# Two steps change places in a decoder kernel: a doubling step ahead of the window's value product, the queries' state product ahead of the second block's inverse

## The chip, the cores and the metric

The kernel runs on one core of a Trainium2 chip. The metric is the device time of one execution in microseconds (us). An execution has a span, from its first to its last recorded instruction, and a little more time around it. The engines are named as in the profile: PE is the matrix engine (TensorE), PEld its loading of stationary operands, DVE the VectorE, ACT the ScalarE, POOL the GpSimd, SP the engine that issues the weight DMAs.

## The reference, cut to what matters

Two layers are computed over 256 tokens of width 1024. Each layer is a half-step SwiGLU, a group of three token mixers that run on the same normalised stream, an output projection and a second half-step SwiGLU, with a layer norm after each. The mixers are a gated DeltaNet, a sliding-window attention with sinks, and a cross-attention to a memory. Their outputs are weighted by sigmoid gates and added:

```python
o_dn = deltanet_branch(dn_q, dn_k, dn_v, dn_b, dn_a, dn_z, ...)
o_sw = sliding_window_attention(sw_q, sw_k, sw_v, swa_sinks)
o_xa = memory_cross_attention(xa_q, mem_n, w_mem_kv)
gates = jax.nn.sigmoid(gates.reshape(B_, S_, N_BRANCH, D))
merged = jnp.sum(gates * jnp.einsum('bsnc,ncd->bsnd', branches, w_branch), axis=2)
```

Two pieces of this matter here. The sliding-window attention multiplies its softmax weights by the values (`o = einsum(p, vb)`). The DeltaNet solves a unit triangular system for every chunk and head and carries a state `S` from chunk to chunk: `v_new = u - w S`, `o = q S + qk v_new`.

## The kernel before, in words

All large products are made from float32 numbers split in two parts. A weight unit of 128 x 1024 arrives by DMA in a tile `raw`; ScalarE rounds it to `whi`, VectorE makes the rest `wlo` (both line 125, in `split`), and three matmuls (line 134, through `mm3`) use `whi` twice and `wlo` once. Four `raw` buffers and five each of `whi` and `wlo` let the conversions run ahead of PE.

Within a mixer group PE's matmuls are pinned to program order (`pinned[0] = True`; products have line 134 in the profile, transposes line 137). That order is written out by hand: `weave(work, steps)` runs a generator of large products, here `gates(n)` (a gate projection in eight steps, each of one weight unit and 12 matmuls) or `branch(n, o)` (a branch projection in four steps), and after step k calls the small pieces that stand under k in a table. The order on DVE and ACT is chosen by a scheduler, the DMA queue of SP keeps program order, and waits between engines follow from the tiles that are shared.

The tokens are handled as two blocks of 128. The small pieces that the change and its steps touch are these:

- `w_scores(tb, hh)` makes the window's scores of one block and half of the heads in `at` banks (a ring of two PSUM banks); DVE reads each bank at line 779 into a tile `pp`, then maximum (785), exponentials on ACT (791), sums (792, 793) and scaling (794). `w_turn` transposes the weights and copies them to `pt` (804).
- `w_values(0)` multiplies the first block's weights `pt` by the values `swv` into one `at` bank (the rows `at<-pt,swv` on PE), and `split` moves it to the two parts of `oS` (ACT and DVE at line 125, the rows `u<-at`).
- `inverses()` builds 16 x 16 inverses on POOL (lines 845 to 847). `begin_inverse` transposes the result on DVE (line 940).
- `doubling(c)` is a generator for each block c that makes larger inverses out of smaller ones; `double()` advances both by one step. The first step is 64 matmuls of 32 x 32 in two `sm` banks (the rows `sm<-w,l`; a ring of two banks as well), each bank copied by ACT at line 884; the second subtracts at line 890 on DVE.
- `rec_v0`, `rec_s1`, `rec_r1`, `rec_o0`, `rec_qs`, `rec_v1`, `rec_o1` are the recurrence: each is four matmuls of 128 x 128 (eight records in the trace) in an `sm` bank and an eviction. `rec_r1` leaves R1 by four DVE operations at line 983; `rec_v1` multiplies the second block's inverse by R1 and is copied by ACT at line 990; `rec_qs` multiplies the queries by the state S1, and DVE evicts it at line 987; `rec_o1` uses V1, and DVE adds it at line 994.

Of the kernel before, what the change touches and what calls it, by code (L numbers as in the profile page):

```python
# [38 lines left out]
def tile_trunk(ctx, tc, x, xT, mem, memT_, wst, lnp, memln, cvw, rows, cst, out):  # L39
# [22 lines left out]
    def T(pool, shape, tag, dt=F32, bufs=None):  # L62
        pool = pn if pool is pu and tag in NEAR else pool
        kw = {} if bufs is None else {"bufs": bufs}
        return pool.tile(shape, dt, tag=tag, name=nm(tag), **kw)
# [4 lines left out]
    def at():  # L70
        return T(psT, [P, 512], "at")
# [52 lines left out]
    def split(hi, lo, src):  # L124
        return nc.scalar.copy(hi, src).ins, nc.vector.tensor_tensor(lo, src, hi.bitcast(F32), op=ALU.subtract).ins  # L125
# [7 lines left out]
    def matmul(*a, **k):  # L133
        return pe(nc.tensor.matmul(*a, **k))  # L134
# [10 lines left out]
    def weave(work, steps):  # L145

        for n, _ in enumerate(work, 1):
            for f in steps.get(n, ()):
                f()
# [374 lines left out]
    def mixers(l, hT, mkT, mv_, post):  # L524
# [281 lines left out]
        def w_values(tb):  # L806
            if not oS:
                oS.extend(T(pu, [P, 4, S], tag, F32R) for tag in ("u6", "u7"))
            ts = slice(tb * P, (tb + 1) * P)
            pso = at()  # L810
            for kb in range(tb + 1):
                for kv in range(2):
                    hs = slice(kv * 64, kv * 64 + 64)
                    matmul(pso[hs, :], swv[:, kb, hs], wpT[tb][kb][:, kv].rearrange("p h q -> p (h q)"), start=kb == 0, stop=kb == tb)
            late["act"], late["dve"] = split(oS[0][:, :, ts], oS[1][:, :, ts], pso.rearrange("p (h k) -> p h k", h=4))
# [189 lines left out]
        def gates(n):  # L1005
            gt = gts[n] = [T(p2, [P, D], "gt") for _ in range(2)]
            for j in range(2):
                js = slice(j * 512, (j + 1) * 512)
                outs = [acc() for _ in range(2)]
                for uu in range(KD // 2):  # L1010
                    hi, lo = unit()
                    for tb in range(2):
                        ts = slice(tb * P, (tb + 1) * P)
                        for kk in range(2):
                            k, c = 2 * uu + kk, slice(kk * 512, kk * 512 + 512)
                            mm3(outs[tb], (xt[0](k)[:, ts], xt[1](k)[:, ts]), (hi[:, c], lo[:, c]), k == 0, k == KD - 1)
                    if uu < KD // 2 - 1:
                        yield
                for tb in range(2):
                    nc.scalar.activation(gt[tb][:, js], outs[tb], AF.Tanh, scale=0.5)  # L1020
                yield

        def branch(n, o):
# [27 lines left out]
            3: [lambda: w_turn(0, 1), begin_inverse],  # L1051
            4: [lambda: w_scores(1, 0)]})
        weave(gates(1), {
            1: [lambda: w_values(0), double],
            2: [lambda: w_scores(1, 1)],
            3: [double, lambda: held(leave_v)],
            5: [double, lambda: w_turn(1, 0), lambda: held(back_v)],
# [7 lines left out]
            4: [rec_r1]})  # L1065
        weave(gates(2), {
            1: [rec_o0],
            2: [rec_v1, rec_qs],
            3: [rec_o1],
            5: [lambda: finish_turn(0)],  # L1070
            8: [lambda: finish_turn(1)]})
# [59 lines left out]
    for l in range(NL):  # L1131
        mT = []
        mid = memory_T(mT, l)
        if l == 0:

            mid[2] = lambda: load(cs, cst)
            more = {4: lambda *a: xres(0), 6: lambda *a: xres(1), 8: lambda *a: small()}
        post = Post(lnp[l, 0, 0], lnp[l, 0, 1])
        f1.rest(hT, 4, [((pu, "u0"), (pu, "u1")), ((pu, "u2"), (pu, "u3"))], post, mid, ends, {} if l else more)
        kv = memory_kv(mT, post.end)  # L1140
        if l == 0:
            nc.scalar.activation(nea, rw[:, :, 8:12], AF.Exp)
            nc.vector.tensor_scalar(nea, nea, -1.0, None, ALU.mult)
        post2 = Post(lnp[l, 1, 0], lnp[l, 1, 1])
        mixers(l, post.hT, *kv, post2)
        f2 = Ffn()
        begin(f2, post2.hT)
        last = l == NL - 1
        post = Post(lnp[l, 2, 0], lnp[l, 2, 1], last)
        f2.rest(post2.hT, 6, [((pu, a), (pu, b)) for a, b in (("u0", "u1"), ("u2", "u3"), ("u4", "u5"), ("u6", "u13"))], post, behind=post2.end)  # L1150
        ends = post.end
        if not last:
            f1, hT = Ffn(), post.hT
            begin(f1, hT)
# [87 lines left out]
```

## Time and profile before

| | |
|---|---|
| median of 3 runs | 1271.19 us (1271.11 to 1272.05) |
| profiled execution, its own time | 1271.84 us |
| its span | 1270.1 us |
| mean granted clock of TensorE | 0.999 |
| DVE, ACT, POOL busy | 69%, 52%, 17% |
| DMA | 263.56 MB, mean 208 GB/s |

A row of the timeline gives the start of an instruction or of a run of equal ones, how long it took, engine, line, operation, output and inputs by the program's names, shape and count, and in brackets how long the engine sat idle before it and what ended that. Matmuls overlap: the next one starts before the row of the last one ends, so that distances on PE are read from start to start. The small pieces of the change stand once in each layer, at about 340 and 395 us in the first layer and at about 970 and 1025 us in the second.

### The profile page before, as it was taken

The numbers are of one execution on the slowest core, as the hardware profiler recorded it, in microseconds if no ns is written. First come the engines' busy times: TensorE is split into PE (matmuls) and PEld (weight loads), VectorE is DVE, ScalarE is ACT, GpSimd is POOL, SyncE is SP. The second block draws the span as 40 slices with busy tenths as digits, with TensorE's granted clock in tenths as the row PEclk, the third lists the DMA queues.
The fourth block names the chain that finished last, engine by engine and source line by source line (L and its number), as shares of the span: only waits on it lengthen the run. The fifth ranks groups of instructions, "written<-read, shape, count | busy, mean of one in ns | idle before, by whom it ended". The sixth has DMA issues, their size and how long they took to land.

```text
span 1270.1 us, 18774 instructions
## 1 busy us (share of the span) xinstructions
PE 1258.1 (99%) x6916; PEld 1070.9 (84%) x6916; DVE 871.3 (69%) x1284; ACT 661.5 (52%) x982; POOL 221.0 (17%) x395
## 2 busy tenths in 40 slices
PE   9999999999999999999999999999999999999997
PEld 7888889999878888888888888899987788888886
DVE  6678576886667776665666665759776588766565
ACT  6456444655664544454454554455646654454441
POOL 1233000002331102221012220000023401122100
PEclk9999999999999999999999999999999999999999
DMA  8988765655554648787668887566554456578771
GB/s 293 322 265 286 249 210 160 205 179 137 164 151 150 240 139 258 243 242 220 215 208 246 256 255 216 178 185 212 162 158 133 134 189 226 174 248 243 240 231 74
DMA packets 78795, 263.56 MB, mean 208 GB/s; under 512 B 12528, under 2 KB 13968, under 8 KB 78704
## 3 DMA queue, kind: packets, MB, share of 16 engines
q1 hardware_dynamic: 66320, 232.40, 56.5%
q0 software_dynamic: 12240, 29.84, 8.7%
q8 instruction: 54, 0.88, 0.3%
q14 instruction: 37, 0.30, 0.1%
q10 hardware_dynamic: 144, 0.13, 0.0%
HBM read 247.48 MB, written 14.85 MB: 207 GB/s over the span
## 4 chain that ended last, share of the span: by engine, by line
PE 94%; DVE 3%; DMA 2%; ACT 1%; issue 1%; SPq 0%; DVEq 0%; ACTq 0%
PE acc L134 83%; PE at L134 3%; PE sm L134 3%; DMA raw<-in_wst_dram 2%; PE sm L137 1%; DVE wlo L125 1%; PE acc L335 1%; PE acc L332 1%; PE at L137 1%; PE acc L333 1%; ACT whi L125 1%; DVE h L291 0%; DVE h L296 0%; DVE h L418 0%; DVE bnst L277 0%
## 5 line engine op out<-in xcount | busy, mean ns | idle before, releaser
L125 DVE TENSOR_TENSOR wlo<-raw,whi 128x1024 fp32r<-128x1024 f32 (+2 forms) x405 | 487.1, 1210 | 277.0 <-ACT whi L125 275.0
L125 ACT CAST whi<-raw 128x1024 fp32r<-128x1024 f32 (+2 forms) x405 | 413.7, 1029 | 403.5 <-PE acc L134 314.8
L134 PE MATMUL acc<-whi,hT 128*128 128x512 f32 (+1 forms) x1824 | 563.1, 386 | 0.0
L134 PEld LDWEIGHTS acc<-whi,hT 128*128 128x128 f32 x1824 | 340.5, 188 | 68.9 <-issue 1.6
L134 PE MATMUL acc<-wlo,hT 128*128 128x512 f32 (+1 forms) x912 | 350.5, 384 | 0.1
L134 PE MATMUL acc<-whi,u 128*128 128x512 f32 x812 | 259.6, 392 | 0.0
L134 PEld LDWEIGHTS acc<-wlo,hT 128*128 128x128 f32 x912 | 171.6, 188 | 33.4 <-DVE wlo L125 0.9
L134 PEld LDWEIGHTS acc<-whi,u 128*128 128x128 f32 x812 | 152.3, 188 | 32.0 <-DVE u L125 0.5
L134 PE MATMUL acc<-wlo,u 128*128 128x512 f32 x406 | 158.2, 390 | 0.0
L362 POOL DMA_DIRECT2D tr<-t x176 | 96.0, 552 | 306.4 <-DVE t L356 299.4
L134 PE MATMUL acc<-hT,whi 128*128 128x256 f32 x672 | 121.8, 284 | 0.0
L134 PEld LDWEIGHTS acc<-hT,whi 128*128 128x128 f32 x672 | 104.7, 192 | 0.0
L134 PE MATMUL acc<-hT,wlo 128*128 128x256 f32 x336 | 95.1, 283 | 0.0
L134 PEld LDWEIGHTS acc<-wlo,u 128*128 128x128 f32 x406 | 76.3, 188 | 15.5
L134 PEld LDWEIGHTS acc<-hT,wlo 128*128 128x128 f32 x336 | 64.4, 192 | 0.0
L363 POOL DMA_DIRECT2D pt<-tr x44 | 25.0, 568 | 197.3 <-DMA tr<-t 151.6
L353 ACT ACTIVATE t<-acc 128x256 f32<-128x256 f32 x88 | 33.3, 379 | 37.1 <-PE acc L134 36.9
L134 PE MATMUL acc<-u,u 128*128 128x512 f32 x186 | 46.4, 394 | 0.0
L354 DVE TENSOR_TENSOR t<-t,acc 128x256 f32<-128x256 f32 x88 | 36.6, 417 | 8.1 <-ACT t L353 3.9
L134 PEld LDWEIGHTS acc<-u,u 128*128 128x128 f32 x186 | 34.6, 188 | 7.5
L553 DVE SCALAR_TENSOR_TENSOR t<-acc,cw,t 128x255 f32<-128x255 f32 (+2 forms) x72 | 34.5, 479 | 1.1
L125 DVE TENSOR_TENSOR u<-pt,u 128x512 fp32r<-128x512 f32 x44 | 28.9, 657 | 8.1 <-ACT u L125 8.1
(245 smaller groups left out, 1165.0 us busy)
## 6 DMA issues: line engine op xcount, KB each, us to landing
raw<-in_wst_dram SPq DMA_DIRECT2D x409, 512.0 KB, 4.4
tr<-t POOLq DMA_DIRECT2D x176, 64.0 KB, 3.9
pt<-tr POOLq DMA_DIRECT2D x44, 256.0 KB, 5.1
raw<-in_wst_dram SPq DMA_DIRECT2D x16, 324.0 KB, 3.0
gB<-in_lnp_dram SPq DMA_DIRECT2D x6, 512.0 KB, 6.7
bB<-in_lnp_dram SPq DMA_DIRECT2D x6, 512.0 KB, 7.0
w<-dr POOLq DMA_DIRECT2D x4, 512.0 KB, 12.6
t<-in_xT_dram SPq DMA_DIRECT2D x4, 256.0 KB, 5.4
```

The source lines that it names most:

```text
L125: return nc.scalar.copy(hi, src).ins, nc.vector.tensor_tensor(lo, src, hi.bitcast(F32), op=ALU.subtract).ins
L134: return pe(nc.tensor.matmul(*a, **k))
L137: return pe(nc.tensor.transpose(*a))
L332: nc.tensor.matmul(ps, hT[0][:, k, ts], hi[:, c], start=k == 0, stop=False)
L333: nc.tensor.matmul(ps, hT[0][:, k, ts], lo[:, c], start=False, stop=False)
L335: nc.tensor.matmul(ps, hT[1][:, k, ts], hi[:, c], start=False, stop=k == KD - 1)
L353: act = nc.scalar.activation(t[:, :, tb, :], g, AF.Silu).ins
L354: ins = nc.vector.tensor_tensor(t[:, :, tb, :], t[:, :, tb, :], u, op=ALU.mult).ins
L362: nc.gpsimd.dma_start(d[:, :, q].rearrange("b c x -> c b x"), z[32 * q:32 * q + 32].rearrange("c (b x) -> c b x", b=4))
L363: back = nc.gpsimd.dma_start(y, d.rearrange("b c q x -> (b c) (q x)")).ins
L553: nc.vector.scalar_tensor_tensor(yc[:, j, d:], b[:, j, :S - d], w[:, t:t + 1], yc[:, j, d:], op0=ALU.mult, op1=ALU.add)
```

## The change

Two entries of the hand-written tables trade places. After the first step of `gates(1)`, the first doubling step of both blocks is issued ahead of `w_values(0)`. After the second step of `gates(2)`, `rec_qs` is issued ahead of `rec_v1`. Nothing is added or taken away.

```diff
         weave(gates(1), {
-            1: [lambda: w_values(0), double],
+            1: [double, lambda: w_values(0)],
             2: [lambda: w_scores(1, 1)],
...
         weave(gates(2), {
             1: [rec_o0],
-            2: [rec_v1, rec_qs],
+            2: [rec_qs, rec_v1],
             3: [rec_o1],
```

On PE, after the first weight unit of the second gate projection in the first layer (`acc` are the large products, `at` the window's value product, `sm` the doubling step):

```order
 L134 MATMUL acc_3424<-wlo_3427,hT_1602 128x512
 L134 MATMUL acc_3424<-whi_3426,hT_1602 128x512
-L134 MATMUL at_3445<-pt_3350,swv_2063 64x512 x2
-L134 MATMUL sm_3450<-w_466_2584,l_465_2583 32x32 x16
-L134 MATMUL sm_3468<-w_466_2584,l_465_2583 32x32 x16
+L134 MATMUL sm_3443<-w_466_2584,l_465_2583 32x32 x16
+L134 MATMUL sm_3461<-w_466_2584,l_465_2583 32x32 x16
+L134 MATMUL at_3481<-pt_3350,swv_2063 64x512 x2
 L134 MATMUL acc_3423<-whi_3487,hT_1602 128x512
 L134 MATMUL acc_3423<-wlo_3488,hT_1602 128x512
```

The two products of `w_values(0)` now stand behind both halves of the doubling step, directly ahead of the next weight unit. The order on DVE, POOL and SP is the same as before but for tile numbers.

On ACT at the same place (`u` is `oS`, the two copies at line 884 belong to the doubling step, 788 and 791 to the window's scores of the second block):

```order
-L125 CAST u_608_3443<-at_3445 128x4x128 [waits PE_49]
-L884 COPY w_457_2573<-sm_3450 128x4x32 [waits DMASW7_49,PE_49,Pool_49]
-L884 COPY w_458_2574<-sm_3468 128x4x32 [waits DMASW0_49,PE_49,Pool_49]
+L884 COPY w_457_2573<-sm_3443 128x4x32 [waits DMASW7_49,PE_49,Pool_49]
+L884 COPY w_458_2574<-sm_3461 128x4x32 [waits DMASW0_49,PE_49,Pool_49]
+L125 CAST u_610_3479<-at_3481 128x4x128 [waits PE_49]
 L788 ACTIVATE sk_3405<-sk_3405 128x4 [waits DVE_49]
 L791 ACTIVATE pp_3392,sums_3404<-pp_3392,mx_3403 128x256 [waits DVE_49]
-L791 ACTIVATE pp_3392,sums_3404<-pp_3392,mx_3403 128x256
 L125 CAST whi_3734<-raw_3733 128x1024 [waits DMAHW2_49,PE_49,Activation_49]
-L791 ACTIVATE pp_3392,sums_3404<-pp_3392,mx_3403 128x256 x2
+L791 ACTIVATE pp_3392,sums_3404<-pp_3392,mx_3403 128x256 x3
```

The cast of the value product goes behind the two copies, and one weight conversion goes ahead of one more of the four exponentials.

On PE, after the second weight unit of the third gate projection, with the waits that each row carries (the four matmuls of `rec_v1` are those with two tiles `w`, those of `rec_qs` have `u_386`, the queries):

```order
 L134 MATMUL acc_3956<-whi_4004,hT_1602 128x512
-L134 MATMUL sm_4021<-w_458_2574,w_467_2585 128x128 [waits DVE_49,Activation_49]
-L134 MATMUL sm_4021<-w_458_2574,w_467_2585 128x128 x3
-L134 MATMUL sm_4028<-w_458_2574,u_386_2075 128x128 x4
+L134 MATMUL sm_4022<-w_458_2574,u_386_2075 128x128 [waits Activation_49]
+L134 MATMUL sm_4022<-w_458_2574,u_386_2075 128x128 x3
+L134 MATMUL sm_4028<-w_458_2574,w_467_2585 128x128 [waits DVE_49]
+L134 MATMUL sm_4028<-w_458_2574,w_467_2585 128x128 x3
 L134 MATMUL acc_3955<-whi_4035,hT_1602 128x512
```

The wait for DVE moves from the first of these eight matmuls to the fifth. The first matmul of `rec_o1`, one step later, waits for ACT alone before and now. The second layer has the same three places.

## The prediction

> **What bounds the kernel now.** I read the page first, then PE's waits, then the timelines of PE, DVE and ACT around the two places of the change, in both layers.
>
> ```profile
> span 1270.1 us, 18774 instructions
> PE 1258.1 (99%) x6916; PEld 1070.9 (84%) x6916; DVE 871.3 (69%) x1284; ACT 661.5 (52%) x982; POOL 221.0 (17%) x395
> ```
>
> PE has work nearly all the time, so only what PE does or waits for can move the end. Its waits, with what released it, the total, how often, and the longest:
>
> ```profile
> PE sm L1118 <- DVE pp L1115: 1.5, 1, 1.5
> PE at L134 <- DVE pp L779: 1.2, 2, 1.0
> PE sm L137 <- DVE h L296: 0.4, 1, 0.4
> PE sm L134 <- DVE w L983: 0.3, 2, 0.2
> ```
>
> There are six waits in the whole execution. The first is at the very start and the third in a layer norm; the other four, 1.2 and 0.3 us, are at the matmuls that the change moves: the value product (released by DVE line 779, which empties an `at` bank) and `rec_v1` (released by line 983, which makes R1). No wait for a weight unit is among them.
>
> **First place: a doubling step ahead of the value product.** PE in the second layer, then in the first:
>
> ```profile
> 968.91 0.39 PE L134 MATMUL acc<-whi,hT 128*128 128x512 f32 x1
> 970.34 1.08 PE L134 MATMUL at<-pt,swv 128*64 128x512 f32 x4 [1.04 <-DVE pp L779]
> 971.35 1.51 PE L134 MATMUL sm<-w,l 32*32 32x32 f32 x64
> 972.78 0.50 PE L134 MATMUL acc<-whi,hT 128*128 128x512 f32 x1
> ```
>
> ```profile
> 340.41 0.39 PE L134 MATMUL acc<-whi,hT 128*128 128x512 f32 x1
> 340.98 1.08 PE L134 MATMUL at<-pt,swv 128*64 128x512 f32 x4 [0.18 <-DVE pp L779]
> ...
> 343.42 0.50 PE L134 MATMUL acc<-whi,hT 128*128 128x512 f32 x1
> ```
>
> From the last matmul of one weight unit to the first of the next it takes 972.78 - 968.91 = 3.87 us in the second layer and 343.42 - 340.41 = 3.01 us in the first. Of that the value product holds PE from its start for 971.35 - 970.34 = 1.01 us and the doubling step for 972.78 - 971.35 = 1.43 us. What such a step costs behind a large product when nothing is late is seen one step on:
>
> ```profile
> 350.22 0.39 PE L134 MATMUL acc<-whi,hT 128*128 128x512 f32 x1
> 350.54 1.51 PE L134 MATMUL sm<-w,w 32*32 32x32 f32 x64
> ```
>
> That is 0.32 us from start to start. With the doubling step first the stretch is 0.32 + 1.43 + 1.01 = 2.76 us, if neither step waits: 3.87 - 2.76 = 1.11 us less in the second layer, 3.01 - 2.76 = 0.25 us less in the first. Without the wait the value product may also take less than 1.01 us, so that a tenth more is possible in each; a changed order of tile shapes could cost as much.
>
> Does neither wait? On DVE:
>
> ```profile
> 340.24 1.28 DVE L779 SCALAR_TENSOR_TENSOR pp<-at,cs 128x512 f32<-128x512 f32 x2
> ...
> 964.73 0.45 DVE L940 STREAM_TRANSPOSE w<-w 128x256 f32<-128x256 f32 x1 [4.93 <-POOL w L847]
> 965.09 4.59 DVE L125 TENSOR_TENSOR wlo<-raw,whi 128x1024 fp32r<-128x1024 f32 x4
> 969.60 1.28 DVE L779 SCALAR_TENSOR_TENSOR pp<-at,cs 128x512 f32<-128x512 f32 x2
> ```
>
> The doubling step needs line 940, which ends at 965.18; PE would come at 968.91 + 0.32 = 969.23, so 4.05 us are in hand. The value product would come at 969.23 + 1.43 = 970.66. It needs the first half of the pair at line 779, whose two operations end together at 970.88: if it got the bank of the second half, it would wait 0.2 us, else nothing (in the first layer 341.52 against 342.16). A later POOL chain delays lines 940 and 779 together, since 779 stands behind 940 and four conversions on DVE; so the old order always waits longer than the new one.
>
> What is queued behind the moved steps? The two copies at line 884 come earlier, and nobody needs them before the doubling step a weight unit later. The cast of the value product comes later, DVE's part of the split waits for it, and the bank of both is needed by the second product of the next window's scores (`at<-swk,u`):
>
> ```profile
> 971.46 0.58 ACT L125 CAST u<-at 128x512 fp32r<-128x512 f32 x1 [0.46 <-PE at L134]
> ...
> 973.26 0.68 DVE L125 TENSOR_TENSOR u<-at,u 128x512 fp32r<-128x512 f32 x1
> ...
> 976.34 0.63 PE L134 MATMUL at<-swk,u 128*128 128x512 f32 x2
> ```
>
> ```profile
> 343.90 0.69 DVE L125 TENSOR_TENSOR u<-at,u 128x512 fp32r<-128x512 f32 x1
> ...
> 346.98 0.63 PE L134 MATMUL at<-swk,u 128*128 128x512 f32 x2
> ```
>
> The cast starts 971.46 - 970.34 = 1.12 us after the product; that would be 970.66 + 1.12 = 971.78, ending at 972.36. DVE has other work until 973.26, so its part does not move. It ends at 973.94, and PE would want the bank at 976.34 - 1.11 = 975.23: 1.29 us in hand. In the first layer the cast would end at 342.16 + 1.12 + 0.58 = 343.86, just ahead of 343.90, and 346.98 - 0.25 - 344.59 = 2.14 us are in hand. The conversion that ACT makes one exponential earlier is work ahead of need: no row of the waits names a conversion. I put it at nothing.
>
> **Second place: the queries' product ahead of `rec_v1`.** PE in both layers, one piece that waits for nothing (`rec_o0`), and DVE's line 983:
>
> ```profile
> 390.86 0.39 PE L134 MATMUL acc<-whi,hT 128*128 128x512 f32 x1
> 391.08 1.05 PE L134 MATMUL sm<-w,u 128*128 128x128 f32 x8
> 391.89 0.48 PE L134 MATMUL acc<-whi,hT 128*128 128x512 f32 x1
> ...
> 394.50 0.39 PE L134 MATMUL acc<-whi,hT 128*128 128x512 f32 x1
> 395.05 1.13 PE L134 MATMUL sm<-w,w 128*128 128x128 f32 x8 [0.15 <-DVE w L983]
> 396.01 1.06 PE L134 MATMUL sm<-w,u 128*128 128x128 f32 x8
> 396.82 0.48 PE L134 MATMUL acc<-whi,hT 128*128 128x512 f32 x1
> ...
> 1023.86 0.39 PE L134 MATMUL acc<-whi,hT 128*128 128x512 f32 x1
> 1024.41 1.13 PE L134 MATMUL sm<-w,w 128*128 128x128 f32 x8 [0.16 <-DVE w L983]
> ...
> 1026.19 0.48 PE L134 MATMUL acc<-whi,hT 128*128 128x512 f32 x1
> ```
>
> ```profile
> 394.31 0.59 DVE L983 SCALAR_TENSOR_TENSOR w<-sm,neg,u 128x128 f32<-128x128 f32 x2
> ```
>
> The pair takes 396.82 - 394.50 = 2.32 us and 1026.19 - 1023.86 = 2.33 us. A piece that does not wait starts 391.08 - 390.86 = 0.22 us after the large product and lasts 391.89 - 391.08 = 0.81 us, so two of them take 0.22 + 2 x 0.81 = 1.84 us: 0.48 and 0.49 us less. R1 is ready at 394.90; with the queries' product first, `rec_v1` starts at 394.50 + 0.22 + 0.81 = 395.53, so 0.63 us are in hand. Its copy then moves back by 395.53 - 395.05 = 0.48 us, while the gain has brought the rest forward; `rec_o1`, which needs it, stands here:
>
> ```profile
> 399.53 0.68 DVE L987 TENSOR_TENSOR t<-sm,eg 128x512 f32<-128x512 f32 x1
> ...
> 399.66 1.05 PE L134 MATMUL sm<-w,u 128*128 128x128 f32 x8
> ```
>
> That is three microseconds after `rec_v1`, so the copy is not late.
>
> Of each wait's price a part is not idle time: `rec_v1` takes 396.01 - 395.05 = 0.96 us instead of 0.81, because its weights are loaded as late as the matmul:
>
> ```profile
> 395.01 0.97 PEld L134 LDWEIGHTS sm<-w,w 128*128 128x128 f32 x8 [0.55 <-issue]
> ```
>
> [...] The row at 390.86 (0.39 us long, the next start 0.22 us on) agrees that idle time behind such rows is counted too small, so I use starts alone.
>
> **The sum.** 1.11 + 0.25 + 0.48 + 0.49 = 2.33 us. Against the profiled execution's own time: 1271.84 - 2.33 = 1269.5 us. The median of the runs is 0.65 us lower. If that has nothing to do with the waits, the median falls to 1271.19 - 2.33 = 1268.9 us. If the quicker runs were quicker because POOL was earlier in the second layer and the wait there shorter, as it is in the first, the gain on the median is 2.33 - 0.65 = 1.7 us. I take the middle, 1269.2 us. What follows is paced by PE, and the only later waits are relative to it, so nothing swallows the gain. A measurement of this kernel can tell about 0.2% (2.5 us) from no change; the forecast, 0.16%, lies inside.
>
> **The rivals.**
>
> 1. *The wait was long only in the profiled run.* If both layers have the first layer's 0.25 us, the gain is 2 x 0.25 + 0.97 = 1.47 us: 1269.7 us. For it: the two layers differ by 0.86 us in the same code. Chance 0.15.
> 2. *The wait is longer in other runs.* With 1.11 us in both layers: 2 x 1.11 + 0.97 = 3.2 us, so 1268.0 us. Chance 0.08.
> 3. *The gain turns into a wait at `rec_o1`.* Were its bank that of the queries' product, PE would wait for line 987 until 400.21 instead of starting at 399.66 - 0.48 = 399.18: about 1.0 us in each layer, 0.3 us left: 1270.9 us. Against it: `rec_o1` waits for ACT alone in the new order, and line 987 is DVE's. Chance 0.08, with all other waits of such a size.
> 4. *The queries' product waits for line 983 as well*, having got `rec_r1`'s bank; then the second place gains nothing, and 1.36 us are left: 1269.8 us. Against it: its row waits for ACT alone. Chance 0.04.
> 5. *Slower: the late cast holds DVE and then PE.* The place is the second score product (346.98 and 976.34 us). If the split of the value product came behind four more conversions (the row with 4.59 us), PE would wait 4.59 - 1.29 = 3.30 us in the second layer and 4.59 - 2.14 = 2.45 us in the first: 5.75 - 2.33 = 3.4 us slower, 1274.6 us. It outweighs the gain once the split is about 2.9 us late in both layers (1.6 + 0.8 us of waits). For it: ACT's queue does put two copies ahead of the cast. Against it: DVE's order stays as it is and DVE has other work at that time. Chance 0.05.
>
> **How the numbers follow.** The forecast has 0.60. About a third of it lies beyond 2.5 us, because its upper reading is 1268.9 us and a tenth of a microsecond is open in each of the four terms: 0.20, with rival 2 makes 0.28 for faster. Rival 5 is the 0.05 for slower. The rest is 0.67. The range goes from 1267.8 us (rival 2, two tenths under it) to 1270.9 us (rival 3).
>
> **What would show it.** In the changed kernel's trace the four waits at lines 779 and 983 are gone from PE's list. The distance between the weight units is 2.76 us at the first place in both layers and 1.84 us at the second. The cast `u<-at` follows the two copies at line 884, and DVE's split of it starts at the same distance behind line 785 as before. It would be wrong if a new PE wait shows: for line 940 at the doubling step, for line 125 at `at<-swk,u`, for line 987 at `rec_o1`, or for a conversion anywhere. The sum would be wrong if the distances come out as forecast and the time does not follow.

## The result and the profile after

The median of the changed kernel is 1269.42 us (19 runs, 1268.64 to 1270.91), that of the kernel before, on the same chip, 1271.34 us (19 runs). The ratio is 0.9984 with a 95% interval of 0.9978 to 0.9991: about 1.9 us less (1.1 to 2.8 us), below the 2.5 us that the prediction called no change, but with an interval that leaves 1 out. The forecast was 1269.2 us. The profiled execution took 1269.55 us by its own time, 2.29 us less than that of before.

The head of the page after, then PE's two longest waits (total, times, longest):

```profile
span 1267.8 us, 18770 instructions
PE 1257.0 (99%) x6916; PEld 1070.2 (84%) x6916; DVE 870.5 (69%) x1284; ACT 661.0 (52%) x982; POOL 221.7 (17%) x395
```

```profile
PE sm L1118 <- DVE pp L1115: 1.5, 1, 1.5
PE acc L134 <- ACT whi L125: 0.8, 2, 0.6
```

The four waits for DVE lines 779 and 983 are gone. The waits for `whi` stand within the first ten microseconds of the execution, and a later profile of the kernel before (`e8_before_again` below) has two like them, 1.0 us, so they are not the change's. PE at the two places, first layer, then second (these rows count records, two to a matmul: the 64 of the doubling step are the 32 matmuls of the order listing):

```profile
340.95 0.39 PE L134 MATMUL acc<-whi,hT 128*128 128x512 f32 x1
341.27 1.51 PE L134 MATMUL sm<-w,l 32*32 32x32 f32 x64
342.71 1.08 PE L134 MATMUL at<-pt,swv 128*64 128x512 f32 x4
343.72 0.50 PE L134 MATMUL acc<-whi,hT 128*128 128x512 f32 x1
...
394.81 0.39 PE L134 MATMUL acc<-whi,hT 128*128 128x512 f32 x1
395.04 1.05 PE L134 MATMUL sm<-w,u 128*128 128x128 f32 x8
395.93 1.06 PE L134 MATMUL sm<-w,w 128*128 128x128 f32 x8
396.74 0.48 PE L134 MATMUL acc<-whi,hT 128*128 128x512 f32 x1
...
399.56 1.05 PE L134 MATMUL sm<-w,u 128*128 128x128 f32 x8
...
968.12 0.39 PE L134 MATMUL acc<-whi,hT 128*128 128x512 f32 x1
968.44 1.51 PE L134 MATMUL sm<-w,l 32*32 32x32 f32 x64
969.87 1.08 PE L134 MATMUL at<-pt,swv 128*64 128x512 f32 x4
970.88 0.50 PE L134 MATMUL acc<-whi,hT 128*128 128x512 f32 x1
...
974.45 0.63 PE L134 MATMUL at<-swk,u 128*128 128x512 f32 x2
...
1021.98 0.39 PE L134 MATMUL acc<-whi,hT 128*128 128x512 f32 x1
...
1023.91 0.48 PE L134 MATMUL acc<-whi,hT 128*128 128x512 f32 x1
```

From weight unit to weight unit the first place takes 343.72 - 340.95 = 2.77 us and 970.88 - 968.12 = 2.76 us, where it took 3.01 and 3.87 us. The second takes 396.74 - 394.81 = 1.93 us and 1023.91 - 1021.98 = 1.93 us, where it took 2.32 and 2.33 us. That is 0.24 + 1.11 + 0.39 + 0.40 = 2.14 us.

Where the rest of the 2.3 us between the two spans lies is read from the starts of equal rows: PE is 0.54 us later than in before at 340 us (340.95 against 340.41), 0.79 us earlier at 968 us (968.12 against 968.91) and 2.28 us earlier at 1024 us. The 0.54 has arisen by 187 us, where neither exchange has run yet. Between 397 and 968 us the changed kernel gains another 0.71 us, of which 0.41 us is the layer norm's wait (line 296), which this execution doesn't have. These two differences lie elsewhere than the change and nearly cancel; the layer norm's wait comes and goes from profile to profile, and neither exchange touches that place (it is there in the runs `e2_queries_first` and `e4_after_slow_bank` below, not in `e1_doubling_first`).

DVE and ACT around the two places:

```profile
394.63 0.60 DVE L983 SCALAR_TENSOR_TENSOR w<-sm,neg,u 128x128 f32<-128x128 f32 x2
...
399.86 0.68 DVE L987 TENSOR_TENSOR t<-sm,eg 128x512 f32<-128x512 f32 x1
...
967.95 1.28 DVE L779 SCALAR_TENSOR_TENSOR pp<-at,cs 128x512 f32<-128x512 f32 x2
...
971.62 0.69 DVE L125 TENSOR_TENSOR u<-at,u 128x512 fp32r<-128x512 f32 x1
```

```profile
971.00 0.59 ACT L125 CAST u<-at 128x512 fp32r<-128x512 f32 x1 [0.71 <-PE at L134]
```

The cast ends at 971.59, DVE's part begins at 971.62: nothing waits, but only 0.03 us are in hand there. DVE's part ends at 972.31, and PE wants the bank at 974.45.

### The profile page after: what moved, and what is told of

It is laid out like the page before. It is cut to its first block, busy times and chain, and to the rows that moved or that the text cites. A ratio compares the mean times of both kernels' runs of the same rounds, so it can differ in the third digit from the quotient of the medians.

```text
span 1267.8 us, 18770 instructions
## 1 busy us (share of the span) xinstructions
PE 1257.0 (99%) x6916; PEld 1070.2 (84%) x6916; DVE 870.5 (69%) x1284; ACT 661.0 (52%) x982; POOL 221.7 (17%) x395
## 4 chain that ended last, share of the span: by engine, by line
PE 99%; DMA 0%; DVE 0%; SPq 0%; ACT 0%; issue 0%; DVEq 0%
PE acc L134 87%; PE at L134 4%; PE sm L134 3%; PE sm L137 1%; PE acc L332 1%; PE acc L333 1%; PE acc L335 1%; PE at L137 1%; DMA raw<-in_wst_dram 0%; DVE h L291 0%; DVE h L296 0%; SPq L115 0%; SPq L78 0%; ACT whi L125 0%; DVE bnst L277 0%
```

## Experiments

Each run has an expectation that was written before it; lengths of "the first place" and "the second place" are distances between weight units as above. Ratios are to runs of the kernel before on the same chip: its median was 1271.27 us beside the first four kernels, 1270.98 us beside the next four, 1271.51 us beside the two with four copies.

### One exchange at a time

`e1_doubling_first` is the kernel before with only the first exchange:

```diff
-            1: [lambda: w_values(0), double],
+            1: [double, lambda: w_values(0)],
```

> Only the first exchange: the doubling step ahead of the value product; rec_v1 stays ahead of rec_qs. Theory (each exchange takes away a PE wait of its own, and PE is the bound): the distance from the last matmul of the first weight unit to the first of the next is 2.76 us in both layers, instead of 3.01 and 3.87 us; the pair of the recurrence keeps its 2.32 us in both layers with the wait for line 983. Time 0.5 to 1.4 us below the kernel before, by the length of the second layer's wait in these runs: ratio 0.9989 to 0.9996. Rival (the gain of the changed kernel lies in its start and its layer norms, which differed from the profile of before by +0.54 and -0.6 us, and not in the exchanges): ratio 1.000.

Measured: median 1270.53 us against 1271.27 us, ratio 0.9994 (0.9985 to 1.0003). The interval includes 1, so that the time alone doesn't rule out the rival; the distances show the gain. The first place takes 2.76 us (343.26 - 340.50) and 2.77 us, the second stays at 2.32 and 2.33 us, and of the four waits these two are left:

```profile
PE sm L134 <- DVE w L983: 0.3, 2, 0.2
```

`e2_queries_first` has only the second exchange:

```diff
-            2: [rec_v1, rec_qs],
+            2: [rec_qs, rec_v1],
```

> Only the second exchange: rec_qs ahead of rec_v1; the value product stays ahead of the doubling step. Theory: the pair takes 1.93 us in both layers as in the changed kernel, instead of 2.32 us, so 0.8 us below the kernel before: ratio 0.9994. The value product keeps its wait, 0.2 us in the first layer and 0.2 to 1.1 us in the second. Rival (start and layer norms): ratio 1.000. The two single exchanges together give the changed kernel's gain if they are independent.

Measured: median 1270.48 us, ratio 0.9991 (0.9982 to 1.0000). The second place takes 1.93 and 1.92 us. The first place, whose order is that of before, holds a surprise in the second layer:

```profile
968.93 0.39 PE L134 MATMUL acc<-whi,hT 128*128 128x512 f32 x1
...
971.94 0.50 PE L134 MATMUL acc<-whi,hT 128*128 128x512 f32 x1
```

It takes 3.01 us here, and took 3.87 us in the profile of before: same order, 0.86 us less wait. 0.9994 x 0.9991 = 0.9985, and both together gave 0.9984, as two independent gains would; the intervals are too wide to prove it. How the two share the gain is not settled by these times (each interval is 0.0018 wide); by the traces the second gives 0.8 us, the first 0.5 to 1.35 us as its wait in the old order was short or long.

### Is it the bank that the value product waits for?

`e3_before_slow_bank` (kernel before) and `e4_after_slow_bank` (changed kernel) do line 779 twice for the two banks that stand ahead of the value product, with the same values:

```diff
+                for _ in range(2 if (tb, hh) == (1, 0) else 1):
                     nc.vector.scalar_tensor_tensor(pr[...], ps..., 0.125, msk..., op0=ALU.mult, op1=ALU.add)
```

> The kernel before, with DVE's line 779 done twice for both banks of the first half of the second block's window scores (the same values are written a second time; four operations of 0.68 us instead of two). By the order on DVE a bank is free after the third of them, about 1.24 us later than before. Theory (PE waits for this release, start to start): the distance at the first place grows by about 1.2 us in each layer, to 4.2 us in the first and 4.2 to 5.1 us in the second; time 2.5 us above the kernel before: ratio 1.002. Rival (the wait is not what costs time, DVE has room): ratio 1.000.

> The changed kernel with the same doubled line 779. In the changed kernel's trace the pair at line 779 ends its first half 1.3 us before the value product starts in both layers (341.4 against 342.71 us, 968.6 against 969.87 us). Theory: the doubling step covers these 1.3 us, so a release 1.24 us later costs 0 to 0.1 us in each layer; the distance stays 2.76 to 2.9 us, the ratio to the kernel before 0.9984 to 0.9986, and the kernel before with the same delay is 4.5 us slower than this one. Rival: DVE's extra 1.3 us per layer are lost here as well, ratio 1.0004.

Measured: 1274.40 us, ratio 1.0020 (1.0011 to 1.0029), and 1270.21 us, ratio 0.9989 (0.9980 to 0.9998). In the old order, second layer (the line is 780 there):

```profile
971.15 1.08 PE L134 MATMUL at<-pt,swv 128*64 128x512 f32 x4 [1.53 <-DVE pp L780]
```

The first place takes 4.21 and 4.37 us in the old order and 2.77 and 2.78 us in the new one. A bank that is released later costs the old order all of it and the new order nothing that shows in its trace: the two medians are 4.19 us apart, where those without the doubling are 1.92 us apart, and the rival of `e4_after_slow_bank` (1.0004) lies outside its interval. The distances of the two traces account for 1.44 + 1.59 us at the first place and 0.8 us at the second, 3.8 us in all; the traced execution of `e3_before_slow_bank` was the quickest of its eleven (1272.70 us). So the wait that the exchange removes is that for the bank, and the doubling step covers it.

### Why was the second layer's wait 3.87 us once and 3.01 us once?

`e8_before_again` is the kernel before once more, for its trace.

> The kernel before once more, for its trace alone. The first place's distance was 3.87 us in the second layer in the first profile of this order and 3.01 us in a later profile of the same order of these steps. My theory: it varies from run to run with the time at which GpSimd ends, between 3.0 and 3.9 us, while the first layer stays at 3.0 us; the time is 1270 to 1273 us. Rival: it is fixed by the kernel's order, and comes out at 3.87 us within 0.05 again.

Its first place takes 3.01 us in the first layer and, in the second:

```profile
969.43 0.39 PE L134 MATMUL acc<-whi,hT 128*128 128x512 f32 x1
...
972.66 0.50 PE L134 MATMUL acc<-whi,hT 128*128 128x512 f32 x1
```

3.23 us: it varies, and the rival (3.87 us again) falls. Back along the chain: POOL's products start when a DMA through DRAM (issued at line 833, tile `w` from `dr`) has landed; in the first layer of the kernel before, the profile gives this DMA as what ended 9.4 us of idle time ahead of them. The DMA view for 930 to 955 us gives its median time from issue to landing in its last column; first the kernel before, then `e8_before_again`, then `e2_queries_first`:

```profile
w<-dr POOLq DMA_DIRECT2D x2, 512.0 KB, 12.9
```

```profile
w<-dr POOLq DMA_DIRECT2D x2, 512.0 KB, 11.9
```

```profile
w<-dr POOLq DMA_DIRECT2D x2, 512.0 KB, 9.4
```

12.9, 11.9 and 9.4 us stand beside 3.87, 3.23 and 3.01 us. POOL's first product starts 12.84, 12.24 and 9.70 us after the issue (950.40 - 937.56, 950.21 - 937.97, 947.30 - 937.60). The DMA is issued 31.3 to 31.5 us ahead of the weight unit's last matmul in all three, and POOL's last product then starts 4.96, 5.61 and 7.95 us ahead of it, so the difference arises between issue and landing. The last distance is the floor: there DVE's conversions wait for ACT's (2.02 us in `e2_queries_first`, 0.77 us in the changed kernel), and line 779 starts 0.17 us ahead of the weight unit's last matmul (968.76 against 968.93), as in the changed kernel (967.95 against 968.12). Why the DMA lands sooner or later was not tested.

### A later POOL chain in both orders

`e5_pool_late_before` and `e7_pool_late_after` copy a tile onto itself eight times on POOL ahead of its last product (2.77 to 2.78 us together); `e9_pool_half_late_before` and `e10_pool_half_late_after` four times (1.35 to 1.36 us). Line 847 of before is line 849 in these:

```diff
+            for _ in range(8):
+                nc.gpsimd.tensor_copy(y16, y16)
             nc.gpsimd.tensor_tensor(Y32..., op=ALU.mult)
```

> The kernel before with GpSimd's chain of inverses made later: ahead of its second product (line 847) it copies the first product onto itself eight times, so that the values stay as they are and the chain ends later by eight such copies, by my estimate 2.5 to 3 us. My theory: the release of the bank at the value product hangs on this chain, through the transpose at line 940 and the operations that stand behind it on DVE. The wait at line 779 then grows wherever the chain was already what DVE waited for: the first place goes from 3.0-3.9 us to 4.5-6.5 us in the second layer and to 3.5-5.5 us in the first, and the median rises by 2 to 5 us, to 1273-1276 us. Rival: the wait at line 779 comes from DVE's conversions of weights, which stand ahead of line 779 and follow the weights and ScalarE; then the distances stay within 0.3 us of 3.0-3.9 and the median stays at 1271.3 us.

> The changed kernel with the same eight copies on GpSimd. My theory: the doubling step (1.43 us) stands between the weight unit and the value product now, and needs line 940, which the chain also delays, but DVE has conversions between line 940 and line 779, so that it comes in time. Of the wait that the kernel before has with these copies, up to about 1.3 us goes at each of the two places: the distance is 1.2 to 1.5 us shorter than there in each layer, or 2.76 us where no wait is left, and with 0.8 us of the second place the median is 2.5 to 4 us below that of the kernel before with the copies. Rival: the late chain holds the doubling step itself, at line 940, so that the new order waits as long as the old one; then the distances of the two kernels agree within 0.3 us, a wait of PE for line 940 appears, and the medians differ by 0.8 us or less.

Measured: 1278.61 us, ratio 1.0060 (1.0047 to 1.0073), and 1272.56 us, ratio 1.0004 (0.9994 to 1.0013). The sign was right in `e5_pool_late_before` and the size was not: 7.6 us where 2 to 5 were expected. The two medians are 6.05 us apart, also more than the 2.5 to 4 expected. PE in `e5_pool_late_before` in the second layer, POOL's last product, and the windows view (after PEld, DVE, ACT and POOL comes the granted clock):

```profile
969.69 0.39 PE L134 MATMUL acc<-whi,hT 128*128 128x512 f32 x1
974.44 1.98 PE L134 MATMUL at<-pt,swv 128*64 128x512 f32 x4 [4.36 <-DVE pp L779]
976.34 2.31 PE L134 MATMUL sm<-w,l 32*32 32x32 f32 x64
978.59 0.80 PE L134 MATMUL acc<-whi,hT 128*128 128x512 f32 x1
```

```profile
968.05 0.74 POOL L849 TENSOR_TENSOR w<-t,cs 128x256 f32<-128x256 f32 x1
```

```profile
975.00:980.00 5.00, 5.00 (x71) 3.34 (x68) 3.27 (x6) 2.16 (x9) 0.00 (x0) 0.50 0.85 274
```

Two things came together. The DMA landed late in this execution (14.6 us), so that the wait was 4.36 us; and after it the granted clock stood at 0.50. The value product took 976.34 - 974.44 = 1.90 us instead of 1.01, the doubling step 2.25 instead of 1.44, the weight unit after it about 2.1 us more than before. The first place took 8.90 us here, and 4.18 us in the first layer, where PE waited 1.34 us and the clock stayed at 1.00.

In `e7_pool_late_after` PE, first layer and one row of the second; then the windows of the two layers:

```profile
340.17 0.39 PE L134 MATMUL acc<-whi,hT 128*128 128x512 f32 x1
340.49 1.51 PE L134 MATMUL sm<-w,l 32*32 32x32 f32 x64
343.29 1.65 PE L134 MATMUL at<-pt,swv 128*64 128x512 f32 x4 [1.30 <-DVE pp L779]
344.87 0.80 PE L134 MATMUL acc<-whi,hT 128*128 128x512 f32 x1
...
973.47 1.08 PE L134 MATMUL at<-pt,swv 128*64 128x512 f32 x4 [1.30 <-DVE pp L779]
```

```profile
340.00:345.00 5.00, 3.70 (x72) 1.85 (x70) 4.97 (x6) 1.39 (x4) 0.00 (x0) 0.87 0.81 274
...
970.00:975.00 5.00, 3.70 (x74) 2.34 (x73) 4.97 (x6) 1.78 (x4) 0.00 (x0) 1.00 0.87 267
```

The doubling step starts 0.32 us after the weight unit as ever, so the rival (a wait for line 940) falls. The expected distance, 1.2 to 1.5 us shorter than in the old order in each layer, did not come: 4.70 us in the first layer against 4.18, and 4.14 us in the second against 8.90. The comparison was a bad one, since the copies don't fix where the chain ends relative to PE: POOL's last product started 336.89, that is 3.28 us ahead of 340.17, and in `e5_pool_late_before` 335.93, 4.66 us ahead of 340.59. What holds in both orders is a rule of starts. Where DVE's conversions follow line 940 at once, line 779 starts 5.65 to 5.67 us after POOL's last product (before: 963.95 and 969.60; `e5_pool_late_before`: 968.05 and 973.70; `e7_pool_late_after`: 336.89 and 342.56), and the value product 0.73 to 0.74 us after that. From there to the next weight unit the old order has 1.01 + 1.43 us of work and the new one 1.01 us. For an equally late chain the new order thus gains, by this rule, the doubling step's 1.43 us, and less where the chain is early enough; what the clock adds comes on top.

The two runs with four copies put that to the times:

> The kernel before with four copies instead of eight on GpSimd (1.4 us by the rows of eight, 2.78 us). My theory: DVE's pair at line 779 starts at the later of two times, 0.17 us ahead of the last matmul of the weight unit, or 5.65 us after the start of GpSimd's last product; the value product starts 0.74 us after that, and the distance at the first place is that start plus 2.44 us. GpSimd's last product started 7.2 us (first layer) and 5.0 to 5.6 us (second layer) ahead of that matmul in the profiles of the kernel before; 1.4 us later is 5.8 and 3.6 to 4.2 us ahead. The distance would be 3.0 to 3.1 us in the first layer and 4.6 to 5.3 us in the second, and the median rises by 1 to 2 us, to 1272-1273.3 us, more if the idle time lowers the granted clock. Rival: the order of the steps does not matter for a late chain, and this kernel differs from the changed kernel with the same copies by no more than the 1.9 us of the kernels without them.

> The changed kernel with four copies on GpSimd. My theory: by the same rule for DVE's pair, and with the doubling step covering 1.75 us after the weight unit's last matmul, the value product waits only where GpSimd's last product starts less than 4.6 us ahead of that matmul. The distance stays at 2.76 us in the first layer and lies between 2.76 and 3.8 us in the second; the median stays at 1269.4 to 1270.2 us, 2.3 to 3.7 us below the kernel before with the same copies. Rival: the doubling step itself waits for line 940, or the two orders suffer alike; then the difference is 1.9 us or less.

Measured: 1272.28 us, ratio 1.0008 (0.9995 to 1.0020), and 1269.43 us, ratio 0.9988 (0.9979 to 0.9996). The medians are 2.85 us apart, inside the 2.3 to 3.7 expected; but the two intervals, about 3.2 and 2.2 us wide, don't exclude the rival's 1.9 us. The traces show the gain. Second layer of `e9_pool_half_late_before`, then of `e10_pool_half_late_after`:

```profile
969.61 0.39 PE L134 MATMUL acc<-whi,hT 128*128 128x512 f32 x1
970.82 1.08 PE L134 MATMUL at<-pt,swv 128*64 128x512 f32 x4 [0.81 <-DVE pp L779]
...
973.26 0.50 PE L134 MATMUL acc<-whi,hT 128*128 128x512 f32 x1
```

```profile
968.03 0.39 PE L134 MATMUL acc<-whi,hT 128*128 128x512 f32 x1
...
970.80 0.50 PE L134 MATMUL acc<-whi,hT 128*128 128x512 f32 x1
```

3.65 us against 2.77 us; in the first layers 3.29 against 2.76 us. The expected 4.6 to 5.3 us in the old order's second layer was too much, again because the DMA landed earlier in this execution (10.9 us); by the rule, POOL's 964.42 gives 970.07 for line 779, and it started at 970.08. The first layer's 3.29 us is above the 3.0 to 3.1 expected: POOL's last product started 5.55 us ahead there, not 5.8, and by the rule that gives 3.28 us. No wait of PE for line 940 shows in either layer of the new order.

### The second place's missing tenth

`e6_pieces_apart` is the changed kernel with the three pieces in three gaps:

```diff
-            2: [rec_qs, rec_v1],
-            3: [rec_o1],
+            2: [rec_qs],
+            3: [rec_v1],
+            4: [rec_o1],
```

> The changed kernel with the three pieces of the second place in three gaps instead of two: the queries' product after step 2 of gates(2), the product with the second inverse after step 3, the second output after step 4. My theory: the pair took 1.93 us instead of 1.84 because its first piece holds PE for 0.89 us when a small piece follows and for 0.81 us when a large product follows; apart, each piece takes 0.81 us, but a further return from large to small products costs PE's start 0.22 us against about 0.05 less in the large product that follows. So the three together come out within 0.15 us of the changed kernel in each layer, and the median at 1269.1 to 1269.6 us, no difference that the times can show. Rival: what was 0.89 us was a hidden wait for line 983; then the product with the second inverse, a weight unit later, gains 0.09 us in each layer and nothing is paid for the further gap. A new wait of PE at one of the three pieces would speak against both.

Measured: 1269.30 us, ratio 0.9984 (0.9975 to 0.9992), as the changed kernel. PE in the second layer, from `rec_o0` to the next transposes (line 137), first in `e6_pieces_apart`, then in the changed kernel:

```profile
1017.96 1.05 PE L134 MATMUL sm<-w,u 128*128 128x128 f32 x8
...
1021.61 1.05 PE L134 MATMUL sm<-w,u 128*128 128x128 f32 x8
1022.42 0.48 PE L134 MATMUL acc<-whi,hT 128*128 128x512 f32 x1
...
1025.24 1.05 PE L134 MATMUL sm<-w,w 128*128 128x128 f32 x8
1026.05 0.48 PE L134 MATMUL acc<-whi,hT 128*128 128x512 f32 x1
...
1032.52 0.60 PE L137 MATMUL sm<-cs,t 128*128 128x128 f32 x4
```

```profile
1018.56 1.05 PE L134 MATMUL sm<-w,u 128*128 128x128 f32 x8
...
1033.10 0.60 PE L137 MATMUL sm<-cs,t 128*128 128x128 f32 x4
```

Apart, each piece holds PE for 0.81 us; as a pair, the first held it for 0.89 us (395.93 - 395.04). But the whole stretch has the same work in both kernels, and it takes 1032.52 - 1017.96 = 14.56 us here and 1033.10 - 1018.56 = 14.54 us in the changed kernel (14.56 and 14.54 us in the first layer as well). Nothing is gained.

The 0.08 us come back in the large product behind the piece. The next start comes 0.31 us after it (1022.42 and 1022.73), where large products behind large ones start 0.23 us apart. So a small piece costs about 0.89 us in either place, and 0.08 us of it shows behind its last matmul: in the distance to the next small piece, or in the large product that follows. A distance that ends at the first large product leaves out the last piece's 0.08 us.

My theory, no difference beyond 0.15 us, held; its price for a further gap, 0.22 us, did not, since a large product's start lies 0.23 us behind the last one anyway. The rival, a hidden wait for line 983 and so a gain, falls by the equal stretches; in the changed kernel R1 is ready at 395.23, 0.7 us ahead of the row at 395.93. Why PE loses these 0.08 us stays open.

## Why the prediction was right, point by point

- **The first place.** 2.76 us in both layers, made of 0.32 + 1.43 + 1.01, as the rows of before had it: gains of 1.11 and 0.24 us against 1.11 and 0.25. That the doubling step covers the bank's release was shown apart, by the doubled line 779. Of the 1.11 us, 0.86 come from the late DMA of that one execution of before, since the old order's floor is 3.01 us. In the profile after, POOL's last product starts at 961.40; 961.40 + 5.65 = 967.05 is ahead of line 779's start at 967.95, so by the rule of starts the old order would have taken the floor there, and the exchange would have gained 0.25 us.
- **The second place.** The term was too large by 0.09 us in each layer: 0.39 and 0.40 us against 0.48 and 0.49. The step at fault is "lasts 0.81 us, so two of them take 0.22 + 2 x 0.81": the row of `rec_o0` was of a piece followed by a large product, and one followed by another small piece took 0.89 us. The reading of the old row fails with it. `rec_v1` took 0.96 us, and the prediction put the 0.15 us above 0.81 down to weights that are loaded late; as the first of the pair without a wait a piece takes 0.89 us, so only 0.07 us went with the wait.
- **Which reading of the median.** 1.92 us lies between the two that were given, 1.7 and 2.33 us, and its interval, 1.1 to 2.8 us, holds both, so that the middle came out so close (1269.2 against 1269.42 us) is in part luck. The two exchanges alone gave 0.74 and 0.79 us, 1.5 us together. The reason was right in part. The second layer's wait does vary from run to run with POOL's end, and the profile of before had the longest of three with that order; that this explains the 0.65 us between that execution and the first median was not shown.
- **Rival 1** (only the first layer's wait in both, 1.47 us) happened in the trace of `e2_queries_first`, and the interval of the median doesn't exclude it. **Rival 2** (a longer wait, 3.2 us) lies outside that interval; a longer wait was made by force with the copies on POOL. The rival was priced without the clock: in `e5_pool_late_before` about 3.8 us were lost on top of a wait of 4.36 us.
- **Rival 3.** `rec_o1` starts at 399.56, before line 987 begins (399.86): it does not wait for that bank. **Rival 4.** `rec_qs` starts at 395.04, before R1 is ready (395.23). **Rival 5.** The cast came later as worked out (971.00 - 969.87 = 1.13 us after its product), DVE's part did not move against line 779 (971.62 - 967.95 = 3.67 us, before 3.66), and PE finds 974.45 - 972.31 = 2.14 us in hand.
- **What would show it wrong.** One sign came by its letter: a wait for a conversion, the 0.8 us for `whi`. It stands in the first ten microseconds and in the old order too, so it says nothing of the change. No wait for line 940, for line 987 or at `at<-swk,u` appeared.
- **The listed waits and the starts.** The second place gained 0.39 us where the wait was listed at 0.15. Between starts PE was idle 0.55 - 0.23 = 0.32 us longer than without the wait, 0.17 us more than listed, and 0.07 us went within the piece. At the first place the value product takes 1.01 us with the wait and without, so there nothing went within the piece. That the prediction went by starts alone was right: 1.5 us of listed waits were 2.14 us between starts.

## What to carry to other kernels

When an engine that has work all the time waits for a buffer, look for a piece with other inputs that can stand ahead of the waiting one; its length is the cover, and the gain is about the smaller of cover and wait: here a piece of 1.43 us took 0.25 and 1.11 us away whole, and 1.44 and 1.59 us where the bank came later. Read such a gain from starts, between two instructions that the change doesn't touch, since the listed idle time begins only at the end of the last matmul's row (0.39 us long, where the next start can come after 0.23 us). Ask of the wait what it hangs on and whether that varies: here it hung on a DMA that landed after 9.4 to 14.6 us in the second layer, so one profile could not say what the median would gain. The order that covers the wait also took less harm from a chain made late on POOL (with eight copies its ratio went from 0.9984 to 1.0004, that of the old order from 1 to 1.0060).

## What the runs showed that was not expected

- **The granted clock was lower after some of the waits.** After 4.36 us of waiting the granted clock was 0.50 for 975 to 980 us, and about 3.8 us were lost on top of the wait (0.89 in the value product, 0.81 in the doubling step, 2.1 in the unit behind). All five executions of `e5_pool_late_before` had a mean clock of 0.994 to 0.996, against 0.998 in the profile `e8_before_again` beside them. In `e7_pool_late_after`, after 1.30 us, it fell in one layer (0.87 over 340 to 345 us, the value product 1.58 us long) and not in the other (1.00, 1.01 us). Its eleven executions fall in two groups: five at a mean clock of 0.996 took 1272.56 to 1273.37 us, five at 0.998 or 0.999 took 1269.24 to 1270.99 us, and one at 0.999 took 1273.77 us; so its median hangs on how often the clock fell. Why it fell after 1.30 us in one layer and not in the other was not tested.
- **A small piece costs 0.08 us more than the distance to the large product behind it shows** (0.89 against 0.81 us); that product's successor starts that much later.
